# Winograd quarter products of a ConvFFN up-projection: two chain tiles kept in the residual's room, and a new order of the products

## The chip, the cores and the metric

The kernel runs on one core of a Trainium2 chip. The metric is the device time of one execution in microseconds (us). A time is compared as the median of several runs; the profiled execution is one run among them and has a time of its own.

## The reference, cut to what matters

Two post-norm layers over x of shape (512, 1024), float32. Each layer has a mixer (attention-like heads in layer 0, state-space heads in layer 1), then a gated ConvFFN. The change lies in the ConvFFN and its surroundings:

```python
def conv_ffn(x, w_up, conv_w, conv_b, w_down):
    h = causal_dwconv(x @ w_up, conv_w, conv_b)      # w_up (1024, 2*2816), conv of width 3
    val, gate = jnp.split(h, 2, axis=-1)
    return (jax.nn.silu(gate) * val) @ w_down        # w_down (2816, 1024)

x = layer_norm(ALPHA * x + y, ln1_g[layer], ln1_b[layer])     # y: the mixer's output
f = conv_ffn(x, ffn_w_up[layer], ffn_conv_w[layer], ffn_conv_b[layer], ffn_w_down[layer])
x = layer_norm(ALPHA * x + f, ln2_g[layer], ln2_b[layer])
```

## The kernel before, in words

Every float32 product is made of three passes of rounded parts: a weight block of 128x1024 is loaded (by SP's queue), split into `hi` (ScalarE, `ACT hi L285`) and `lo` = block - hi (VectorE, `DVE lo L286`), and TensorE multiplies hi x hi, lo x hi and hi x lo of the activations. `hi` and `lo` come from pools of five buffers each (`wp`), plainly loaded blocks from a pool of four (`raw`, in `rp`).

The up-projection of one layer makes 22 pairs of 128 columns (a gate tile g and a value tile v for each j from 0 to 21), in `up_quarters`. j = 0 and 1 are plain: `gated(j, ...)` calls `mtile` twice (24 matmuls of 512 columns each), then `conv` (one ScalarE pass, two VectorE passes, line L988) and the gate. After that come seven groups. A group is two j made together by a Winograd scheme (seven quarter products in place of eight, 24 matmuls of 256 columns each, line L1055), followed by one plain j (not after the last group). In the groups A11, A12, A22 are quarters of the activations; E, S2, S3, S4 are sums of quarters, made once at the start of the stage (E and S2 by VectorE; S3 and S4 by GpSimd at lines L1027 to L1033 and then split).

The weights of four of the seven products are sums of quarter blocks W11, W12, W21, W22. They are summed by accumulating DMAs that GpSimd issues (`nc.gpsimd.dma_start(c, ..., accum_op=add)`): one tile `c` goes through W11, +W12, +W22, +W21, and each addition may start only when the sum before it is split. The tile `c` has one buffer (tag "t", which the tile of S2 and S4 shares), so the W11 of the next group is loaded when the last sum of this one is split. A second sum, d = W12 + W22, uses one of the four `raw` buffers. Products of a group in order: c=W11 with A11 (PSUM x), W21 with A12, c+W12 with E (PSUM y, held to the end), c+W22 with S2 (added onto x in PSUM), c+W21 with A22 (its own PSUM banks tp and av), d with S3 (onto x), W22 with S4 (onto y). Then comes the plain j.

`proj_ln` makes the mixer's output projection, the residual sum and the layer norm, in four row blocks t; the residual stays in four SBUF tiles `xk` (tag "x" of `rp`) until the down-projection adds to it. The norm of each t has two small GpSimd steps (L314, L315). The down-projection, also `proj_ln`, takes each activation block split by `two` into tiles `s` of a pool that is opened when the up-projection's pool is closed.

The order on each engine is made at build time by a scheduler; each engine runs its instructions strictly in that order, so an instruction that waits holds all that stand behind it.

Of the kernel before, what the change touches and what calls it, by code (L numbers as in the profile page):

```python
# [8 lines left out]
F32 = mybir.dt.float32  # L9
F32R = mybir.dt.float32r  # L10
AF = mybir.ActivationFunctionType
# [95 lines left out]
def trunk(ctx: ExitStack, tc: tile.TileContext, W, x, xT, cols, rows, poolw, consts, out):  # L107
# [15 lines left out]
    def nm(s):  # L123
        uid[0] += 1
        return f"{s}_{uid[0]}"

    def ps(tag="mm"):
        return pp.tile([P, 512], F32, tag=tag, name=nm(tag), bufs={"mm": 4, "S": 2, "tp": 1, "av": 1}[tag])
# [43 lines left out]
    def wraw():  # L172
        return rp.tile([P, D], F32, tag="raw", name=nm("raw"), bufs=4)
# [139 lines left out]
    def rpow(dst, var):  # L313
        G.tensor_scalar(dst, var, EPS, None, ALU.add)  # L314
        return G.tensor_tensor(dst, dst, phalf.to_broadcast(list(dst.shape)) if dst.shape[-1] > 1 else phalf, ALU.pow)  # L315

    def proj_ln(acts, korder, blk, ln, nxt, needs=None, scale=None):


# [85 lines left out]
        for t in range(NT):  # L405
            if t + 1 < ahead:
                last(t + 1)
            elif t >= ahead:
                last(t)
            mv = small([P, 2])  # L410
            V.bn_aggr(mv, st[t][:, 0:4 if fine(t) else 2].rearrange("p a b -> p (a b)"))  # L411
            rs = small([P, 1])
            last_pow = rpow(rs, mv[:, 1:2]).ins
            for h in range(2):
                z = xk[t][:, h * 512:(h + 1) * 512]
                V.scalar_tensor_tensor(z, z, mv[:, 0:1], gain[h], ALU.subtract, ALU.mult)
                for c in (slice(0, 256), slice(256, 512)) if fine(t) and h else (slice(0, 512),):
                    V.scalar_tensor_tensor(z[:, c], z[:, c], rs, shift[h][:, c], ALU.mult, ALU.add)  # L418
                    if nxt is None:
                        nc.sync.dma_start(out[t * P:(t + 1) * P, h * 512 + c.start:h * 512 + c.stop], z[:, c])  # L420
            if nxt is None:
                continue
            if t == NT - 1:

                xcur = xnew
                hi, lo, raw = wload(nxt)
                o = ps()
                mpass(o, hi, lo, 3 * P)
            xf = []
            for h in range(2):  # L430
                z = xk[t][:, h * 512:(h + 1) * 512]
                tp = ps()
                for k in range(4):
                    T.transpose(tp[:, k * P:(k + 1) * P], z[:, k * P:(k + 1) * P], ident)
                split(tp.rearrange("p (a b) -> p a b", b=P), xnew[h][:, :, t * P:(t + 1) * P],
                      xnew[2 + h][:, :, t * P:(t + 1) * P])
                if t == NT - 1:
                    xf.append(tmp())
                    A.activation(xf[h], tp, AF.Copy)
# [540 lines left out]
    def ffn(pool, layer, up, dn, last):  # L980
        cw, cb = C_FW[layer], C_FB[layer]
        act = [pool.tile([P, 2, S], F32, tag="a", name=nm("a"), bufs=NJ // 2) for _ in range(NJ // 2)]

        def conv(j, o):
            c = tmp()
            A.activation(c, o, AF.Identity, bias=c1(cb + j), scale=c1(cw + 2 * 2 * NJ + j))  # L986
            for d in range(1, 3):
                V.scalar_tensor_tensor(c[:, d:], o[:, :S - d], c1(cw + (2 - d) * 2 * NJ + j), c[:, d:],  # L988
                                       ALU.mult, ALU.add)
            return c  # L990

        def gated(j, g, v):
            gt = conv(NJ + j, g())
            A.activation(gt, gt, AF.Silu)
            vl = conv(j, v())
            V.tensor_tensor(act[j // 2][:, j % 2, :], vl, gt, ALU.mult)

        with tc.tile_pool(name=f"up{layer}", bufs=1, side="left") as work:
            up_quarters(work, up, gated)
        after_ln[:] = [None, 0]  # L1000
        with tc.tile_pool(name=f"dn{layer}", bufs=1, side="left") as work:
            def two(b):
                hi, lo = (work.tile([P, 2, S], F32R, tag="s", name=nm("s"), bufs=11) for _ in range(2))
                split(act[b], hi, lo, G)
                return [(hi[:, i, :], lo[:, i, :]) for i in range(2)]
            proj_ln(two, range(NJ), dn, 2 * layer + 1, None if last else OD)

    def up_quarters(pool, up, gated):
# [36 lines left out]
        def wsplit(p):  # L1045
            hi = wp.tile([P, D], F32R, tag="hi", name=nm("hi"), bufs=5)
            lo = wp.tile([P, D], F32R, tag="lo", name=nm("lo"), bufs=5)
            split(p, hi, lo)
            return hi, lo

        def mul(o, w, half, a, start=True):
            n = 0
            for ww, part in ((w[0], 0), (w[1], 0), (w[0], 1)):
                for k in range(4):
                    T.matmul(o[:, L], ww[:, half * 512 + k * P:half * 512 + (k + 1) * P], a[part][:, k, :],  # L1055
                             start=start and n == 0, stop=n == 11, skip_group_check=not start)
                    n += 1

        for j in range(3, NJ, 3):
            js = (j - 1, j)  # L1060
            W11, W12, W21, W22 = (W[up + 2 * (j - 1) + i] for i in range(4))
            if j == 3:
                for i in range(4):
                    sl = slice(i, i + 1)
                    total(G, e[:, sl], [(1, [a[:, sl] for a in A11]), (-1, [a[:, sl] for a in A21])])
                    split(e[:, sl], *(a[:, sl] for a in S3))
                S4 = wide("e", F32R), wide("f", F32R)
                for i in range(4):
                    sl = slice(i, i + 1)
                    more(G, s2[:, sl], s2[:, sl], [a[:, sl] for a in A12], ALU.subtract)  # L1070
                    split(s2[:, sl], *(a[:, sl] for a in S4))
            c = pool.tile([P, D], F32, tag="t", name=nm("t"), bufs=1)
            nc.sync.dma_start(c, W11)
            e21, d, e22 = wraw(), wraw(), wraw()
            nc.sync.dma_start(e21, W21)
            nc.sync.dma_start(d, W12)
            nc.sync.dma_start(e22, W22)
            nc.gpsimd.dma_start(d, W22, accum_op=ALU.add)  # L1078
            g = [pool.tile([P, S], F32, tag="g", name=nm("g"), bufs=2) for _ in js]
            v = [pool.tile([P, S], F32, tag="v", name=nm("v"), bufs=2) for _ in js]  # L1080
            x = [ps("S") for _ in js]
            w = wsplit(c)
            for i in range(2):
                mul(x[i], w, i, A11)
                A.activation(g[i][:, L], x[i][:, L], AF.Copy)
            nc.gpsimd.dma_start(c, W12, accum_op=ALU.add)
            w = wsplit(e21)
            for i in range(2):
                o = ps()
                mul(o, w, i, A12)  # L1090
                V.tensor_tensor(g[i][:, L], g[i][:, L], o[:, L], ALU.add)
            w = wsplit(c)
            y = [ps() for _ in js]
            for i in range(2):
                mul(y[i], w, i, E)
                A.activation(v[i][:, R], y[i][:, L], AF.Copy, scale=-1.0)
            nc.gpsimd.dma_start(c, W22, accum_op=ALU.add)
            w = wsplit(c)
            for i in range(2):
                mul(x[i], w, i, S2, False)  # L1100
                A.activation(v[i][:, L], x[i][:, L], AF.Copy)
            nc.gpsimd.dma_start(c, W21, accum_op=ALU.add)
            w = wsplit(c)
            for i in range(2):
                o = ps(("tp", "av")[i])
                mul(o, w, i, A22)
                A.activation(g[i][:, R], o[:, L], AF.Copy)
            w = wsplit(d)
            for i in range(2):
                mul(x[i], w, i, S3, False)  # L1110
                V.tensor_tensor(g[i][:, R], g[i][:, R], x[i][:, L], ALU.add)
                V.tensor_tensor(v[i][:, R], v[i][:, R], x[i][:, L], ALU.subtract)
            w = wsplit(e22)
            for i in range(2):
                mul(y[i], w, i, S4, False)
                V.scalar_tensor_tensor(v[i][:, L], v[i][:, L], -1.0, y[i][:, L], ALU.mult, ALU.subtract)
                gated(js[i], lambda: g[i], lambda: v[i])
            if j + 1 < NJ:
                gated(j + 1, lambda: mtile(up + 2 * j + 2), lambda: mtile(up + 2 * j + 3))

    with tc.tile_pool(name="ev", bufs=1, side="left") as pool:
        even_mixer(pool)
# [119 lines left out]
```

## Time and profile before

| | before |
|---|---|
| median of 3 runs | 1319.55 us (1314.46 to 1319.63) |
| the profiled execution's own time | 1314.97 us |
| its span, first to last instruction | 1313.2 us |
| TensorE (PE) matmuls busy | 1182.9 us, 90% |
| VectorE (DVE) busy | 835.2 us, 64% |
| ScalarE (ACT) busy | 563.1 us, 43% |
| GpSimd (POOL) busy | 327.9 us, 25% |
| mean granted TensorE clock | 0.943 of full |

The granted clock has two levels, 1.2 and 2.4 GHz (0.5 and 1.0). Times on the profile's timeline count from the span's start. The two up-projections lie at about 270 to 563 us (layer 0) and 870 to 1169 us (layer 1).

### The profile page before, as it was taken

The numbers are of one execution on the slowest core, as the hardware profiler recorded it, in microseconds if no ns is written. First come the engines' busy times: TensorE is split into PE (matmuls) and PEld (weight loads), VectorE is DVE, ScalarE is ACT, GpSimd is POOL, SyncE is SP. The second block draws the span as 40 slices with busy tenths as digits, with TensorE's granted clock in tenths as the row PEclk, the third lists the DMA queues.
The fourth block names the chain that finished last, engine by engine and source line by source line (L and its number), as shares of the span: only waits on it lengthen the run. The fifth ranks groups of instructions, "written<-read, shape, count | busy, mean of one in ns | idle before, by whom it ended". The sixth has DMA issues, their size and how long they took to land. (4 is left out here: it accounts for less than half of the span.)

```text
span 1313.2 us, 16580 instructions
## 1 busy us (share of the span) xinstructions
PE 1182.9 (90%) x6320; PEld 1009.4 (77%) x6320; DVE 835.2 (64%) x1282; ACT 563.1 (43%) x889; POOL 327.9 (25%) x330
## 2 busy tenths in 40 slices
PE   8999999994989898969999999996789889959997
PEld 6777788874878888858887766775778889858886
DVE  5977565693656665654547978596456576663545
ACT  4456532142444544453324477224444345453330
POOL 1223222152000110154422075035101110106442
PEclk9999999997989898979999999997789899989999
DMA  8323422233656555543323242313555556652311
GB/s 283 111 91 106 144 72 83 62 81 64 153 153 161 141 137 129 120 149 96 97 64 121 63 147 65 113 33 88 131 119 132 140 150 156 154 157 75 97 49 64
DMA packets 45648, 149.34 MB, mean 114 GB/s; under 512 B 5096, under 2 KB 5736, under 8 KB 45568
## 3 DMA queue, kind: packets, MB, share of 16 engines
q1 hardware_dynamic: 37344, 118.38, 27.5%
q0 software_dynamic: 8224, 29.89, 13.2%
q8 instruction: 50, 0.82, 0.2%
q14 instruction: 30, 0.25, 0.1%
HBM read 146.11 MB, written 2.15 MB: 113 GB/s over the span
## 5 line engine op out<-in xcount | busy, mean ns | idle before, releaser
L286 DVE TENSOR_TENSOR lo<-raw,hi 128x1024 fp32r<-128x1024 f32 (+1 forms) x187 | 250.8, 1356 | 157.2 <-ACT hi L285 157.0
L238 PE MATMUL mm<-xT,hi 128*128 128x512 f32 (+1 forms) x1088 | 281.7, 400 | 0.5 <-ACT xT L285 0.5
L285 ACT ACTIVATE hi<-raw 128x1024 fp32r<-128x1024 f32 (+1 forms) x189 | 186.2, 996 | 190.8 <-PE mm L334 110.5
L238 PEld LDWEIGHTS mm<-xT,hi 128*128 128x128 f32 x1088 | 201.9, 191 | 44.6 <-issue 4.4
L286 DVE TENSOR_TENSOR lo<-t,hi 128x1024 fp32r<-128x1024 f32 x56 | 68.6, 1225 | 194.4 <-ACT hi L285 194.4
L286 POOL TENSOR_TENSOR s<-a,s 128x1024 fp32r<-128x1024 f32 x44 | 107.2, 2446 | 142.0 <-PE mm L334 72.9
L334 PE MATMUL mm<-hi,s 128*128 128x512 f32 (+1 forms) x396 | 121.6, 387 | 22.7 <-ACT s L285 20.3
L285 ACT ACTIVATE hi<-t 128x1024 fp32r<-128x1024 f32 x56 | 59.5, 1062 | 189.9 <-DMA t<-in_W 189.9
L238 PE MATMUL mm<-xT,lo 128*128 128x512 f32 (+1 forms) x544 | 138.8, 391 | 0.0
L238 PEld LDWEIGHTS mm<-xT,lo 128*128 128x128 f32 x544 | 101.0, 188 | 21.4 <-issue 1.9
L334 PEld LDWEIGHTS mm<-hi,s 128*128 128x128 f32 x396 | 75.4, 194 | 38.5 <-issue 20.6
L1055 PE MATMUL S<-o,hi 128*128 128x256 f32 x448 | 76.3, 308 | 6.6 <-ACT hi L285 6.6
L334 PE MATMUL mm<-lo,s 128*128 128x512 f32 (+1 forms) x198 | 76.4, 386 | 0.0
L1055 PEld LDWEIGHTS S<-o,hi 128*128 128x128 f32 x448 | 68.9, 219 | 7.3 <-ACT hi L285 7.3
L1055 PE MATMUL mm<-o,hi 128*128 128x256 f32 x224 | 44.6, 335 | 32.3 <-DVE tmp L988 29.0
L1055 PEld LDWEIGHTS mm<-o,hi 128*128 128x128 f32 x224 | 38.3, 239 | 34.5 <-issue 30.7
L1078 POOL DMA_DIRECT2D raw<-in_W x14 | 12.3, 876 | 192.6 <-DMA raw<-in_W 74.3
L1055 PE MATMUL S<-xT,hi 128*128 128x256 f32 x224 | 36.6, 300 | 24.6 <-ACT hi L285 24.6
L334 PE MATMUL S<-hi,s 128*128 128x512 f32 x176 | 56.9, 390 | 0.0
L314 POOL TENSOR_SCALAR small<-small 128x1 f32<-128x1 f32 (+2 forms) x25 | 14.5, 579 | 163.1 <-DVE small L411 101.7
L1055 PEld LDWEIGHTS S<-xT,hi 128*128 128x128 f32 x224 | 33.3, 208 | 26.4 <-ACT hi L285 25.5
L988 DVE SCALAR_TENSOR_TENSOR tmp<-mm,col,tmp 128x511 f32<-128x511 f32 (+1 forms) x64 | 47.2, 745 | 7.9 <-ACT tmp L986 7.4
(296 smaller groups left out, 2322.9 us busy)
## 6 DMA issues: line engine op xcount, KB each, us to landing
raw<-in_W SPq DMA_DIRECT2D x176, 512.0 KB, 4.1
t<-in_W POOLq DMA_DIRECT2D x42, 512.0 KB, 5.4
raw<-in_W POOLq DMA_DIRECT2D x14, 512.0 KB, 6.8
t<-in_W SPq DMA_DIRECT2D x14, 512.0 KB, 3.4
bc<-dr SPq DMA_DIRECT2D x20, 256.0 KB, 3.9
tmp<-in_rows SPq DMA_DIRECT2D x16, 256.0 KB, 4.1
raw<-in_W SPq DMA_DIRECT2D x8, 256.0 KB, 5.8
xk<-in_x SPq DMA_DIRECT2D x4, 512.0 KB, 5.8
```

Of the source, the lines that this page charges most:

```text
L238: T.matmul(o[:, :cols_], w[:, k * P:(k + 1) * P], xs_(xcur, part, k)[:, :cols_], start=n == 0, stop=n == 3 * NK - 1)
L285: A.activation(hi, src, AF.Copy)
L286: (lo_eng or V).tensor_tensor(lo, src, r32(hi), ALU.subtract)
L314: G.tensor_scalar(dst, var, EPS, None, ALU.add)
L334: T.matmul(o[:, c], a[:, t * P:(t + 1) * P], ww[:, kk * 512 + c.start:kk * 512 + c.stop], start=first and kk == 0 and n == 0, stop=fin and ...
L988: V.scalar_tensor_tensor(c[:, d:], o[:, :S - d], c1(cw + (2 - d) * 2 * NJ + j), c[:, d:], ALU.mult, ALU.add)
L1055: T.matmul(o[:, L], ww[:, half * 512 + k * P:half * 512 + (k + 1) * P], a[part][:, k, :], start=start and n == 0, stop=n == 11, skip_group ...
L1078: nc.gpsimd.dma_start(d, W22, accum_op=ALU.add)
```

## The change

The chain tile c and the sum d move from the up-projection's pool and from `raw` into the tag "x" of `rp`, the four buffers in which the residual lay. A group takes two of the four, so two groups' chains can stand side by side. The residual is written to a DRAM tensor `away` by SP as each row block's norm is done, and loaded back for the down-projection. The plain j moves from behind the group into its middle, between the product with E and that with S2. The product with A22 becomes the last of the group and is added onto x in PSUM, after S2 and S3, so that PSUM makes a sum that VectorE made (L1111 goes; the banks tp and av are not used). The first two activation blocks of the down-projection are split into `hi`/`lo` buffers of `wp` and not into tiles `s`.

```diff
+    away = dp.tile([NT, P, D], F32, name="away")
 ...
             if nxt is None:
                 continue
+            if needs:
+                nc.sync.dma_start(away[t], xk[t])
 ...
         after_ln[:] = [None, 0]
+        for t in range(NT):
+            xk[t] = rp.tile([P, D], F32, tag="x", name=nm("xk"), bufs=4)
+            nc.sync.dma_start(xk[t], away[t])
         with tc.tile_pool(name=f"dn{layer}", bufs=1, side="left") as work:
+            early = [0, 1]
+
             def two(b):
-                hi, lo = (work.tile([P, 2, S], F32R, tag="s", name=nm("s"), bufs=11) for _ in range(2))
+                if early:
+                    early.pop()
+                    hi, lo = (wp.tile([P, D], F32R, tag=g, name=nm("s"), bufs=5).rearrange("p (a b) -> p a b", a=2)
+                              for g in ("hi", "lo"))
+                else:
+                    hi, lo = (work.tile([P, 2, S], F32R, tag="s", name=nm("s"), bufs=11) for _ in range(2))
 ...
-            c = pool.tile([P, D], F32, tag="t", name=nm("t"), bufs=1)
+            c, d = (rp.tile([P, D], F32, tag="x", name=nm("c"), bufs=4) for _ in range(2))
             nc.sync.dma_start(c, W11)
-            e21, d, e22 = wraw(), wraw(), wraw()
+            e21, e22 = wraw(), wraw()
+            nc.sync.dma_start(d, W12)
             nc.sync.dma_start(e21, W21)
-            nc.sync.dma_start(d, W12)
             nc.sync.dma_start(e22, W22)
 ...
             nc.gpsimd.dma_start(c, W22, accum_op=ALU.add)
+            if j + 1 < NJ:
+                gated(j + 1, lambda: mtile(up + 2 * j + 2), lambda: mtile(up + 2 * j + 3))
             w = wsplit(c)
             for i in range(2):
                 mul(x[i], w, i, S2, False)
                 A.activation(v[i][:, L], x[i][:, L], AF.Copy)
             nc.gpsimd.dma_start(c, W21, accum_op=ALU.add)
-            w = wsplit(c)
-            for i in range(2):
-                o = ps(("tp", "av")[i])
-                mul(o, w, i, A22)
-                A.activation(g[i][:, R], o[:, L], AF.Copy)
             w = wsplit(d)
             for i in range(2):
                 mul(x[i], w, i, S3, False)
-                V.tensor_tensor(g[i][:, R], g[i][:, R], x[i][:, L], ALU.add)
                 V.tensor_tensor(v[i][:, R], v[i][:, R], x[i][:, L], ALU.subtract)
             w = wsplit(e22)
             for i in range(2):
                 mul(y[i], w, i, S4, False)
                 V.scalar_tensor_tensor(v[i][:, L], v[i][:, L], -1.0, y[i][:, L], ALU.mult, ALU.subtract)
+            w = wsplit(c)
+            for i in range(2):
+                mul(x[i], w, i, A22, False)
+                A.activation(g[i][:, R], x[i][:, L], AF.Copy)
                 gated(js[i], lambda: g[i], lambda: v[i])
-            if j + 1 < NJ:
-                gated(j + 1, lambda: mtile(up + 2 * j + 2), lambda: mtile(up + 2 * j + 3))
```

Where the instructions stand now. First place: GpSimd's queue from the last norm step of layer 0's mixer to the end of the first group. `raw_2784` is the d of before, `t_2781` its c; a DMA row of GpSimd is an accumulating DMA. Before:

```order
L191 TENSOR_TENSOR lo_2604<-raw_2601,hi_2603 128x1024
L1078 DMA raw_2784<-in_W 128x1024
L1027 TENSOR_TENSOR e_2650<-xT_2348 128x256 x2
L1029 TENSOR_TENSOR e_2650<-e_2650,xT_2350 128x256 x4
...
L1033 TENSOR_TENSOR t_2651<-t_2651,xT_2351 128x256 x2
L1086 DMA t_2781<-in_W 128x1024
L1097 DMA t_2781<-in_W 128x1024
L1102 DMA t_2781<-in_W 128x1024
L1078 DMA raw_3114<-in_W 128x1024
```

And of the change, in the same place (`c_2786` is the c of the first group, `c_2787` its d, `c_3113` the d of the second):

```order
L1092 DMA c_2787<-in_W 128x1024
L314 TENSOR_SCALAR small_2531<-small_2529 128x1
L315 TENSOR_TENSOR small_2531<-small_2531,phalf 128x1
L191 TENSOR_TENSOR lo_2609<-raw_2606,hi_2608 128x1024
L1092 DMA c_3113<-in_W 128x1024
L1100 DMA c_2786<-in_W 128x1024
L1041 TENSOR_TENSOR e_2655<-xT_2349 128x256 x2
...
L1111 DMA c_2786<-in_W 128x1024
L1046 TENSOR_TENSOR t_2656<-t_2656,xT_2350 128x256 x2
...
L1118 DMA c_2786<-in_W 128x1024
L1092 DMA c_3437<-in_W 128x1024
```

The first d now stands ahead of the last row block's two norm steps, and c's additions stand ahead of and among the sums of quarters, not behind them.

Second place: ScalarE where one group gives way to the next, in the middle of layer 0's up-projection. `g` and `v` are the group's outputs, `S` the PSUM tile x, `mm` a plain tile or y. Before (group with `t_3767`, then that with `t_4095`):

```order
L1101 ACTIVATE v_3779<-S_3781 128x256
L285 ACTIVATE hi_4061<-raw_4059 128x1024
L1107 ACTIVATE g_3776<-tp_3913 128x256
L1107 ACTIVATE g_3777<-av_3927 128x256
L285 ACTIVATE hi_4110<-t_4095 128x1024
L285 ACTIVATE hi_4141<-raw_4097 128x1024
L986 ACTIVATE tmp_3990<-g_3776,col 128x512
```

And of the change (`c_3760` is this group's chain, `c_4084` the next one's; `raw_4195` is the next plain g tile's weights):

```order
L990 ACTIVATE tmp_3938<-mm_3913,col 128x512
L285 ACTIVATE hi_4099<-c_4084 128x1024
L1117 ACTIVATE v_3771<-S_3773 128x256
L1117 ACTIVATE v_3772<-S_3774 128x256
L285 ACTIVATE hi_4130<-raw_4087 128x1024
L285 ACTIVATE hi_4162<-c_4084 128x1024
L285 ACTIVATE hi_4197<-raw_4195 128x1024
L1130 ACTIVATE g_3769<-S_3773 128x256
L990 ACTIVATE tmp_4051<-g_3769,col 128x512
L990 ACTIVATE tmp_4056<-v_3771,col 128x512
L1130 ACTIVATE g_3770<-S_3774 128x256
```

The next chain's W11 and its first sum (W11+W12, `hi_4162`) are now split while this group's S2 to A22 products run, and the copy of this group's last x (L1130) stands behind that second split.

Third place: ScalarE from the last copies of layer 0's last group to the down-projection. Before:

```order
L1107 ACTIVATE g_4761<-av_4911 128x256
...
L986 ACTIVATE tmp_5002<-v_4763,col 128x512
L994 ACTIVATE tmp_4974<-tmp_4974 128x512
L285 ACTIVATE hi_5157<-raw_5155 128x1024
L994 ACTIVATE tmp_4997<-tmp_4997 128x512
L285 ACTIVATE s_5021<-a_2587 128x1024
L285 ACTIVATE s_5059<-a_2588 128x1024
```

And of the change:

```order
L285 ACTIVATE hi_4934<-c_4732 128x1024
L285 ACTIVATE hi_5002<-raw_5000 128x1024
L285 ACTIVATE s_5006<-a_2592 128x1024
L285 ACTIVATE hi_5040<-raw_5038 128x1024
L285 ACTIVATE s_5044<-a_2593 128x1024
L1130 ACTIVATE g_4741<-S_4745 128x256
...
L998 ACTIVATE tmp_4974<-tmp_4974 128x512
L285 ACTIVATE hi_5108<-raw_5106 128x1024
L285 ACTIVATE hi_5142<-raw_5140 128x1024
L285 ACTIVATE s_5078<-a_2594 128x1024
```

Two weight blocks and two activation blocks of the down-projection are split ahead of the last group's last copies; the third activation block stands behind them.

## Rows read from the trace of the kernel before

**Rows 1.** The page's chain that ended last, shares of the span by line

```profile
DMA t<-in_W 9%; PE mm L334 5%; PE S L334 2%; DVE lo L286 2%; DMA raw<-in_W 2%; ACT hi L285 1%; PE tp L334 1%; PE S L1055 1%; DVE tmp L988 1%; PE mm L1055 0%; PE av L334 0%; PE tp L1055 0%; PE av L1055 0%; DVE xk L418 0%; POOL raw L1078 0%
```

**Rows 2.** DMA queues (packets, MB, share) and issues (xcount, size, us to landing)

```profile
q1 hardware_dynamic: 37344, 118.38, 27.5%
q0 software_dynamic: 8224, 29.89, 13.2%
...
raw<-in_W SPq DMA_DIRECT2D x176, 512.0 KB, 4.1
t<-in_W POOLq DMA_DIRECT2D x42, 512.0 KB, 5.4
...
out<-xk SPq DMA_DIRECT2D x7, 256.0 KB, 2.0
```

**Rows 3.** Timeline of PE, layer 1: start us, us, instruction [idle before <-releaser]

```profile
912.20 1.44 PE L1055 MATMUL S<-xT,hi 128*128 128x256 f32 x5 [12.50 <-ACT hi L285]
...
960.25 0.64 PE L1055 MATMUL S<-xT,hi 128*128 128x256 f32 x4
```

**Rows 4.** Timeline of PE, one middle group of layer 1

```profile
1045.28 1.20 PE L1055 MATMUL mm<-o,hi 128*128 128x256 f32 x4 [4.46 <-DVE tmp L988]
...
1057.40 0.64 PE L1055 MATMUL mm<-e,hi 128*128 128x256 f32 x4
...
1060.28 2.00 PE L238 MATMUL mm<-xT,hi 128*128 128x512 f32 x8
...
1071.19 0.64 PE L1055 MATMUL S<-xT,hi 128*128 128x256 f32 x4
```

**Rows 5.** The chain in order of time, same group: start us, us, what

```profile
1060.34 9.45 DMA t<-in_W
...
1070.96 1.24 DVE lo L286
...
1072.48 5.54 DMA t<-in_W
```

**Rows 6.** Windows: stretch us, busy by engine (x), PEclk, DMA share, GB/s

```profile
400.00:410.00 10.00, 7.61 (x59) 7.02 (x59) 6.00 (x8) 4.28 (x8) 0.87 (x1) 1.00 0.33 54
471.00:481.00 10.00, 8.04 (x55) 7.87 (x54) 4.64 (x7) 4.02 (x6) 0.87 (x1) 0.83 0.32 53
1040.00:1050.00 10.00, 5.54 (x30) 5.36 (x30) 3.99 (x6) 2.99 (x5) 0.85 (x1) 0.66 0.39 66
1041.00:1079.00 38.00, 33.26 (x216) 31.19 (x216) 23.23 (x32) 18.06 (x27) 3.44 (x4) 0.91 0.56 139
...
1179.50:1186.50 7.00, 5.79 (x13) 4.12 (x14) 0.00 (x0) 4.62 (x5) 7.00 (x4) 0.51 0.41 143
```

**Rows 7.** Timeline of PE, start of layer 1's down-projection

```profile
1179.48 0.76 PE L334 MATMUL mm<-hi,s 128*128 128x512 f32 x1 [10.08 <-ACT s L285]
```

**Rows 8.** Timeline of PE, the same three places of layer 0

```profile
307.30 1.44 PE L1055 MATMUL S<-xT,hi 128*128 128x256 f32 x5 [12.15 <-ACT hi L285]
...
354.14 0.64 PE L1055 MATMUL S<-xT,hi 128*128 128x256 f32 x4
...
573.17 0.77 PE L334 MATMUL mm<-hi,s 128*128 128x512 f32 x1 [10.22 <-ACT s L285]
```

**Rows 9.** Timeline of DVE and POOL, layer 1's norm and sums of quarters

```profile
862.86 1.41 DVE L418 SCALAR_TENSOR_TENSOR xk<-xk,small,tmp 128x512 f32<-128x512 f32 x2
...
873.96 0.78 POOL L314 TENSOR_SCALAR small<-small 128x1 f32<-128x1 f32 x1 [4.70 <-DVE small L411]
...
904.96 1.40 POOL L1033 TENSOR_TENSOR t<-t,xT 128x256 f32<-128x256 f32 x2
```

**Rows 10.** Timeline of ACT and DVE, a plain tile's conv passes and an x copy

```profile
1042.34 0.76 ACT L986 ACTIVATE tmp<-mm,col 128x512 f32<-128x512 f32 x1
...
1043.60 1.53 DVE L988 SCALAR_TENSOR_TENSOR tmp<-mm,col,tmp 128x511 f32<-128x511 f32 x2
...
1055.09 0.40 ACT L1107 ACTIVATE g<-tp 128x256 f32<-128x256 f32 x1
```

## The prediction

> **What bounds the kernel now.** I read the chain that ended last first: its largest entry is the accumulating DMAs of the chain tile, `t<-in_W` with 9% [rows 1], and in order of time a middle group is one string of addition, split, addition, split [rows 5]. An addition lands 5.54 us after its issue, but 9.45 us when it is issued together with d's [rows 5]; from its landing the ScalarE split and its hand-over take 1.17 us (1069.79 to 1070.96), the VectorE split 1.24, and 0.28 pass until the next addition's issue. With one tile c, the next group's W11 is loaded only when this string is over. So I read TensorE's timeline next, and split each layer's up-projection into three stretches.
>
> First group with its plain j, S1: from the end of j = 1 (912.20 less the 12.50 waited, 899.70) to the next group's first product at 960.25, 60.55 us in layer 1 [rows 3]; in layer 0, 295.15 to 354.14, 58.99 us [rows 8]. Last, the start of the down-projection, S3: TensorE waits 10.08 and 10.22 us [rows 7, 8] and then has 5.79 of 7.00 us busy at half clock [rows 6], so it loses 1.21 us more by waiting and 5.79 x 0.49 = 2.8 by the clock: 14.1 and 14.2 us (layer 0's tail taken as layer 1's). Between them lie groups two to seven, S2: 960.25 to 1169.40 and 354.14 to 562.95, 209.15 and 208.81 us [rows 3, 7, 8].
>
> What S1 and S2 would take if TensorE never waited: a product is 24 matmuls, 2.88 us (1057.40 to 1060.28), a plain j 10.91 (1060.28 to 1071.19) [rows 4]. A group with a plain j is 7 x 2.88 + 10.91 = 31.07 us; S2 has 42 products and five plain j, 175.5 us. So S2 loses 33 us per layer and S1 28 to 29. Each loss shows its cause: in S1 the first c is loaded late, in S2 a wait such as the 4.46 us for a PSUM bank that VectorE's `tmp` pass frees, because that pass stands behind a split that waits for c [rows 4]. The waits also cost clock. In 400 to 410, idle 2.39 us in pieces, the granted clock stayed at 1.00; with 1.96 idle it fell to 0.83, with 4.46 to 0.66 over the 10 us [rows 6], which is 1.7 and 3.4 us lost.
>
> **The first group.** c no longer shares a tile with S2 and S4 and is loaded as soon as the first residual block is away, so the 12 us wait goes. What is late next is S4 and the passes behind it. GpSimd ends its sums of quarters at 906.36 before [rows 9]. It starts them when VectorE has split E, and VectorE now has two weight splits (1.24 each [rows 5]) and four conv passes (1.53 for two [rows 10]) ahead of that, 5.5 us in all; I put GpSimd's end that much later, at 911.9. ScalarE's last copy of S4 and a g copy (0.40 each [rows 10]), then VectorE's adds, free PSUM for the plain tile at about 913.4. TensorE could begin it at 899.7 + 3 x 2.88 = 908.3, so it waits 5.1 us, and I charge 2.2 for the clock, between 1.7 and 3.4. S1 becomes 31.07 + 7.3 = 38.3 us (bounds 32 and 45): **20.7 and 22.2 us less**.
>
> **The middle groups.** Here the plain j hides the addition before S2, and the next c is loaded early. The steps that are left in a row run from the end of the plain j to the next group's first product, which on TensorE are four products, 11.52 us. On the other engines: the conv's ScalarE pass 0.76, two VectorE passes 1.53 [rows 10], the split of the next W11, 1.24, and 0.28 to the issue, the addition of W12, 5.54, ScalarE's split of it 1.17 [rows 5], the next plain tile's `hi`, by the same rows about 1.1, and only then, in ScalarE's order, the copy that frees x, 0.40 [rows 10]: 12.0 us, 0.5 more than TensorE needs. The second half of x follows two conv passes of ScalarE later, which costs some 0.3 more than the product's half of 1.44 covers. So a boundary costs **at least 0.8 us**. At most the addition takes 9.45 us, as it does beside d's: 3.9 more, and with a fall of the clock by 3.4 us it is 8.1. I take 0.9 more for the addition, since SP issues d's load only after the plain tile's, which waits for a buffer that the split before S4 gives back some 12 us into the group; d then lands near 19 us, its addition leaves at about 20 and c's at 23, an overlap of part of the way. Of the clock I add 0.8, half of what the wait of 1.96 us lost, since this wait of 1.7 is a little shorter. That is 2.5 us per boundary, five boundaries, and 1 us in the last group, which has no plain j: S2 takes 175.5 + 13.5 = 189 us, **19.8 and 20.2 less**.
>
> Do the other engines fit a group of 33 to 34 us? VectorE had 23.23 us and ScalarE 18.06 us in 38 [rows 6]; yes. The DMA engines: plain loads took 27.5% of the span for 118.38 MB, 1.6 us per 512 KB of all sixteen, additions 13.2% for 29.89 MB, 3.0 us [rows 2]. Six loads and four additions make 21.7 us of 33.5, so they fit, if not without queueing.
>
> **The down-projection's start.** ScalarE's `s` split waited for the room of the old pool. Now two weight and two activation blocks are split before the last copies, so 48 matmuls (11 us) stand ready; the third activation block needs a weight buffer turned over at 5.6 us, two ScalarE passes and a GpSimd pass, about 11 us, just in time. I charge 1 us (bounds 0 and 5): **13.1 and 13.2 less**.
>
> **What is added.** Per layer four blocks go out and come back: 256 KB lands in 2.0 us, 512 KB of load in 4.1 [rows 2], and nothing but c and d waits for them. c's cover is wide (it is needed at 899.7). d's is thin: its addition stands on GpSimd ahead of the norm step that starts at 873.96 [rows 9]. The second block's norm ends at 864.27 [rows 9]; write and load at 4.1 each bring d at 872.5. That holds by 1.5 us; each us beyond holds the norm, and TensorE behind it, by as much. With one ScalarE split in front of a transposed block I charge 0.5 per layer (bounds 0 and 2). Reloading happens under the down-projection, whose residual is first read after half its products. The two PSUM adds less per group (0.8 us of VectorE) are not on a path: nothing.
>
> **The sum.** 20.7 + 22.2 + 19.8 + 20.2 + 13.1 + 13.2 - 1.0 = 108.2 us off the profiled execution's 1314.97: 1206.8. Its time is 4.6 us under the median of the runs shown, whose spread is 5.2; I leave half of that and forecast **1209 us**.
>
> **Rivals.** *No wait is left* (additions at 5.54, S1 at 36, the start free): boundaries at 0.8 make S2 179.5, the sum 23 + 24.5 + 29.3 + 29.6 + 14.2 + 14.1 - 1 = 134, **1181 us**. For it: the boundary is short by only 0.5; against it: more transfers fall together than before.
>
> *The additions meet other transfers at every boundary.* Each boundary costs 8.1, S2 217, and S1 40: 19 + 20.5 - 8.2 - 7.9 + 26.3 - 1 = 49 us, **1266**. The 9.45 us row speaks for it, the order of SP's loads against it. The Trainium skill, page DMA: Bandwidth & Descriptors, section Issuing engines are not separate DMA queues, says that transfers started by different engines run on the same 16 DMA engines and interleave. By that rule, loads that now come earlier do not come for nothing; the 5.54 and 9.45 us agree with it.
>
> *The second tile does not help*, because splits can run only five products ahead, whatever is loaded: S2 stays as it was, 108.2 - 40 = 68.2 us of the sum stay, **1247**.
>
> *Slower than before*: GpSimd's queue. d's addition of the next group stands ahead of c's; if d's load comes late, every c waits for it, and so does each group. The saving elsewhere is 68.2 us and S2 loses 67 now, so it turns at (68.2 + 67 - 2) / 10 = 13.3 us per boundary, that is with d landing some 14 us later than I place it. At 15, **1332 us**. Only SP's order stands against it: one load that waits for a buffer holds d.
>
> **Chances and range.** The forecast (1188 to 1230) 0.50, no wait 0.18, meeting transfers 0.13, no help 0.07, slower 0.05; 0.07 is left for what I don't see (0.02 faster, 0.04 the same, 0.01 slower). Half a per cent is about what a measurement of this kernel can tell from no change. Faster by more than that: 0.50 + 0.18 + 0.13 + 0.07 + 0.02 = 0.90; the same 0.04; slower 0.06. The range 1174 to 1264 holds the forecast, the third case, most of the first rival and nearly half of the second: about 0.8.
>
> **What would show it.** Right: the first group's wait of 12 us is gone and the second group starts 36 to 40 us after j = 1; the groups come every 32 to 35 us; between A22 and the next A11 a wait of 1 to 2 us, ended by ScalarE's copy to g; the first L334 product without a wait; `c<-in_W` landing in 5.5 to 7 us. Wrong: waits of 4 us at each boundary with additions of 9 us; a GpSimd wait for d's load ahead of c's addition; the last norm step held by d; a wait at the third block of the down-projection.

## The result, and the profile of the changed kernel

The changed kernel takes 1278.4 us (median of 4 runs, 1272.7 to 1282.55), the kernel before on the same chip 1318.0. The ratio is 0.970, with a 95% interval of 0.965 to 0.975: faster by some 40 us, of a forecast 108, and outside the range of 1174 to 1264. Its profiled execution took 1282.55 us with a span of 1280.5, against 1314.97 and 1313.2.

The page of the changed kernel: the start of its chain by line, three kinds of DMA issue, and the costliest group of quarter products (busy, mean ns of one | idle before, and its main releaser). Its first line and its DMA issues answer to [rows 1, 2].

```profile
DMA c<-in_W 7%; PE mm L336 4%; PE mm L238 3%; PE S L1069 3%; PE mm L1069 2%; PE S L336 2%; DVE lo L286 1%; PE tp L336 1%; ACT hi L285 1%; DVE tmp L992 1%; POOL e L1043 1%; PE av L336 0%; POOL e L1041 0%; DMA raw<-in_W 0%; POOL s L286 0%
...
L1069 PE MATMUL S<-xT,hi 128*128 128x256 f32 x448 | 85.1, 333 | 57.2 <-ACT g L1130 52.3
...
raw<-in_W SPq DMA_DIRECT2D x162, 512.0 KB, 3.7
c<-in_W POOLq DMA_DIRECT2D x56, 512.0 KB, 7.1
c<-in_W SPq DMA_DIRECT2D x28, 512.0 KB, 3.9
```

The additions are still the chain's largest entry. Their median is now 7.1 us, c's and d's together; before, c's alone had 5.4, and d's stood in another row of the page. 52.3 us of TensorE's idle time stand in one group: the products A11 and A22, waiting for ScalarE's copy out of x.

Now TensorE's timeline at the ends of the three stretches (start us, us, instruction [idle before <-releaser]), first of layer 0, then of layer 1. They answer to [rows 3, 4, 7, 8].

```profile
294.71 0.52 PE L1069 MATMUL S<-xT,lo 128*128 128x256 f32 x3
...
343.88 0.58 PE L1069 MATMUL S<-xT,hi 128*128 128x256 f32 x1 [6.17 <-ACT g L1130]
...
557.05 0.51 PE L336 MATMUL mm<-hi,s 128*128 128x512 f32 x1
...
886.40 0.40 PE L1069 MATMUL S<-xT,lo 128*128 128x256 f32 x2
...
901.61 1.20 PE L1069 MATMUL mm<-o,hi 128*128 128x256 f32 x4 [8.81 <-DVE tmp L992]
...
933.66 0.58 PE L1069 MATMUL S<-xT,hi 128*128 128x256 f32 x1 [6.25 <-ACT g L1130]
...
1011.12 1.22 PE L1069 MATMUL S<-xT,hi 128*128 128x256 f32 x4 [5.37 <-ACT g L1130]
...
1120.59 1.12 PE L1069 MATMUL S<-xT,hi 128*128 128x256 f32 x8
...
1144.86 0.40 PE L336 MATMUL mm<-hi,s 128*128 128x512 f32 x1
...
1156.64 0.50 PE L336 MATMUL mm<-hi,s 128*128 128x512 f32 x1 [0.69 <-ACT s L285]
...
1160.58 0.73 PE L336 MATMUL mm<-hi,s 128*128 128x512 f32 x2 [3.20 <-POOL s L286]
```

The wait of 12 us for the first c is gone, and so are the 10 us at the down-projection. The groups, however, come 37.8 to 39.1 us apart (343.88 to 498.08 and 933.66 to 1087.35), and at the first five of the six boundaries between groups of each layer TensorE waits 3.8 to 6.3 us, 52.3 in all ten. At the last boundary of each layer, between groups six and seven, it does not wait: the row at 1120.59 holds A22 and A11 back to back. With these rows, and those of the kernel named in the last column, the stretches are:

| stretch, us | before | forecast | after | experiment 2 |
|---|---|---|---|---|
| S1, layer 0 | 58.99 | 38.3 | 49.17 | 40.75 |
| S1, layer 1 | 60.55 | 38.3 | 47.26 | 41.96 |
| S2, layer 0 | 208.81 | 189 | 213.17 | 185.31 |
| S2, layer 1 | 209.15 | 189 | 211.20 | 184.90 |
| end of layer 0's S2 to end of layer 1's j = 1 | 336.75 | 324.0 | 329.35 | 331.13 |
| end of layer 1's S2 to the end | 143.8 | 130.7 | 135.64 | 135.6 |

S2, which was to lose 40 us, has grown by 6.4. What holds a boundary is plain from the chain in order of time around the wait at 1011.12, to be held against [rows 5]:

```profile
998.55 0.54 POOL c L1092
999.09 9.63 DMA c<-in_W
1008.72 0.02 issue
...
1008.80 1.06 ACT hi L285
...
1011.41 6.43 DMA c<-in_W
```

and from the timelines of GpSimd, SP and VectorE of the same stretch. L1092 is d's addition, L1100 c's of W12, L1118 c's of W21; L1089 is d's load; `lo<-c` at 993.09 is the split for A22, at 996.54 that of the next group's W11.

```profile
984.38 0.86 POOL L1118 DMA_DIRECT2D c<-in_W  x1 [10.91 <-DVE lo L286]
998.55 0.86 POOL L1092 DMA_DIRECT2D c<-in_W  x1 [13.30 <-DVE a L1000]
999.09 1.22 POOL L1100 DMA_DIRECT2D c<-in_W  x1
...
1037.36 0.86 POOL L1092 DMA_DIRECT2D c<-in_W  x1 [12.86 <-DMA c<-in_W]
1037.89 1.22 POOL L1100 DMA_DIRECT2D c<-in_W  x1
...
994.34 0.33 SPq L1089 DMA_DIRECT2D c<-in_W  x1
...
993.09 1.23 DVE L286 TENSOR_TENSOR lo<-c,hi 128x1024 fp32r<-128x1024 f32 x1 [1.90 <-ACT hi L285]
...
996.54 1.21 DVE L286 TENSOR_TENSOR lo<-c,hi 128x1024 fp32r<-128x1024 f32 x1
```

The d that is loaded at 994.34, and whose addition leaves at 998.55, belongs to the group after next. The four buffers go round two groups, and they are given out in the order in which they come free: the next-but-one c takes the buffer of this group's d, and the next-but-one d that of this group's c, which comes free only when c has been split for A22, at 994.32. d's load leaves 0.02 us later and takes 3.9 us in the median, and only then does its addition leave (at the next boundary, 1037.36, the row names the load as what it waited for), 0.54 us ahead of c's, which stands behind it on GpSimd. c's addition then takes 9.63 us and not 5.5. W11 of the next group had been split by 997.75: without d, the addition could have landed at about 1003.5. Groups six and seven have no d two groups on, and their boundary has no wait.

### The profile page after: what moved, and what is told of

Its sections match the earlier page's. It is cut to its first block, busy times and chain, and to the rows that moved or that the text cites. A ratio compares the mean times of both kernels' runs of the same rounds, so it can differ in the third digit from the quotient of the medians.

```text
span 1280.5 us, 16455 instructions
## 1 busy us (share of the span) xinstructions
PE 1169.7 (91%) x6320; PEld 1000.5 (78%) x6320; DVE 838.7 (65%) x1254; ACT 563.0 (44%) x889; POOL 335.0 (26%) x330
## 5 line engine op out<-in xcount | busy, mean ns | idle before, releaser
L286 DVE TENSOR_TENSOR lo<-raw,hi 128x1024 fp32r<-128x1024 f32 (+1 forms) x173 | 239.6, 1390 | 128.1 <-ACT hi L285 127.5
L285 ACT ACTIVATE hi<-raw 128x1024 fp32r<-128x1024 f32 (+1 forms) x175 | 172.2, 989 | 168.2 <-PE mm L336 102.4
L286 DVE TENSOR_TENSOR lo<-c,hi 128x1024 fp32r<-128x1024 f32 x70 | 84.3, 1220 | 123.1 <-ACT hi L285 123.1
L285 ACT ACTIVATE hi<-c 128x1024 fp32r<-128x1024 f32 x70 | 73.7, 1056 | 183.6 <-DMA c<-in_W 175.1
L286 POOL TENSOR_TENSOR s<-a,s 128x1024 fp32r<-128x1024 f32 x44 | 119.0, 2719 | 108.0 <-PE mm L336 54.5
L1069 PE MATMUL S<-xT,hi 128*128 128x256 f32 x448 | 85.1, 333 | 57.2 <-ACT g L1130 52.3
L1069 PEld LDWEIGHTS S<-xT,hi 128*128 128x128 f32 x448 | 75.3, 240 | 60.1 <-ACT g L1130 54.4
L992 DVE SCALAR_TENSOR_TENSOR tmp<-mm,col,tmp 128x511 f32<-128x511 f32 (+1 forms) x64 | 47.3, 747 | 51.0 <-ACT tmp L990 50.0
L1069 PE MATMUL S<-o,hi 128*128 128x256 f32 x448 | 65.3, 283 | 1.2 <-ACT v L1117 1.2
L990 ACT ACTIVATE tmp<-mm,col 128x512 f32<-128x512 f32 x32 | 24.6, 776 | 67.7 <-PE mm L238 58.8
L1092 POOL DMA_DIRECT2D c<-in_W x14 | 12.3, 880 | 150.2 <-DMA c<-in_W 62.6
```

Source lines behind the costliest of these rows:

```text
L285: A.activation(hi, src, AF.Copy)
L286: (lo_eng or V).tensor_tensor(lo, src, r32(hi), ALU.subtract)
```

## The experiments

Theory A: the loss comes from d's addition, which stands one place ahead of c's on GpSimd. Rivals: B, two additions in flight slow each other whichever is first; C, the plain loads around it slow c's addition. Every ratio is to runs of the kernel before on the same chip in the same session.

### 1 and 2. d's addition behind c's

`issue_after` queues an instruction behind another of its engine. In the first kernel that is c's addition of W12 of one group on, in the second that of W22; the loads stay as they were.

```diff
-            nc.gpsimd.dma_start(d, W22, accum_op=ALU.add)
+            if j == 3:
+                nc.gpsimd.dma_start(d, W22, accum_op=ALU.add)
+            else:
+                with tc.issue_after(last.ins):
+                    nc.gpsimd.dma_start(d, W22, accum_op=ALU.add)
...
-            nc.gpsimd.dma_start(c, W12, accum_op=ALU.add)
+            last = nc.gpsimd.dma_start(c, W12, accum_op=ALU.add)
```

> The only edit: on GpSimd, d's addition is issued just behind c's addition of W12, no longer just ahead of it; buffers, loads and their order stay. Theory A (the ten waits of 3.8 to 6.3 us between a group's last product and the next group's first, 52 us in all, and the 3.4 us of half clock behind each, come from c's addition sharing its flight with d's, and the one issued first is served first): c's addition lands in 5.5 to 7 us, the waits shrink to 0 to 2 us, and the time is 1200 to 1225 us. Rival B (two additions in flight share the engines, whichever is first): c's addition still takes 8.5 to 10 us, the waits stay at 4 to 6 us, and the time is 1265 to 1285. Rival C (c's addition is slow from the plain loads around it, not from d's): as B here, and the next two kernels change nothing either.

> The only edit: on GpSimd, d's addition is issued behind c's addition of W22, some 8 us after that of W12. Under theory A and under rival B alike c's addition of W12 now flies alone: 5.5 to 7 us, waits of 0 to 2 us at the ten boundaries, 1200 to 1225 us, while d's addition meets that of W22, which the plain j hides. Rival C (plain loads slow c's addition): waits of 4 to 6 us stay, 1260 to 1285 us. A third outcome, waits of 4 us moved to the product with S2, would give 1240 to 1270.

Measured: 1226.6 us, ratio 0.927 (0.924 to 0.930), 1.6 us above the range that I gave theory A, and 1217.1 us, 0.921 (0.920 to 0.923), inside it. The first kernel's chain and GpSimd's timeline (L1104 is c's addition of W12, L1096 d's):

```profile
992.43 5.54 DMA c<-in_W
...
992.43 0.86 POOL L1104 DMA_DIRECT2D c<-in_W  x1 [11.62 <-DVE lo L286]
993.49 0.86 POOL L1096 DMA_DIRECT2D c<-in_W  x1 [0.20 <-issue]
```

and the second's (L1115 is c's addition of W22):

```profile
981.64 5.39 DMA c<-in_W
...
989.73 5.59 DMA c<-in_W
...
989.73 0.86 POOL L1115 DMA_DIRECT2D c<-in_W  x1 [7.22 <-DVE lo L286]
990.27 1.22 POOL L1096 DMA_DIRECT2D c<-in_W  x1
```

With d's addition 1.06 or 0.54 us behind it, c's takes 5.54 and 5.59 us; with d's 0.54 us ahead it took 9.63. Rival B falls: the first one issued is not slowed. Rival C falls for this addition: one plain load leaves just behind it in all three kernels, at 999.77 in the changed one (0.7 us behind) and at 993.90 and 983.35 in these (1.5 and 1.7). Plain loads do cost where three of them surround an addition; the last section has the figures. In the second kernel the group `S<-xT,hi` has 9.9 us idle where it had 57.2.

### 3. d in the buffer that comes free early

```diff
-            nc.sync.dma_start(c, W11)
             e21, e22 = wraw(), wraw()
             nc.sync.dma_start(d, W12)
+            nc.sync.dma_start(c, W11)
```

> The only edit: d's load is issued where c's was and c's where d's was, so that d takes the buffer that the d of two groups before gave back early, and c the one that c gave back last. GpSimd's order stays: d's addition ahead of c's of W12. Theory A: d lands some 9 us earlier, its addition leaves before the boundary and c's flies alone; the waits shrink to 0 to 2.5 us (a plain load now begins where d's began), 1200 to 1230 us. Rival C: the transfer that starts 5 us ahead of c's addition is a load of the same size as before, so c's addition stays slow, 1260 to 1285 us.

Measured: 1234.7 us, 0.934 (0.930 to 0.939), 4.7 us above the range. The order on GpSimd is the old one, but d's addition (L1092) now leaves 4.5 us ahead of c's:

```profile
954.62 0.87 POOL L1092 DMA_DIRECT2D c<-in_W  x1 [7.04 <-DMA c<-in_W]
959.11 0.86 POOL L1100 DMA_DIRECT2D c<-in_W  x1 [3.62 <-DVE lo L286]
...
959.11 7.11 DMA c<-in_W
```

c's takes 7.1 us, and boundaries wait 0 to 3 us. So it is not the order alone, but the order together with a buffer that came free late; undoing either brings most of the gain.

### 4. No addition to d

The diff takes out the line of d's addition.

> d's addition is left out altogether, so the product with S3 uses W12 alone and the output is another one; everything else stays. It is the bound of what d's addition costs: theory A 1195 to 1220 us, the waits at the ten boundaries 0 to 2 us; rival C 1255 to 1280 us with waits of 4 us or more.

Measured: 1214.3 us, 0.919 (0.917 to 0.921); the output is another one, since S3's weights lack W22. That is the bound of all that d's addition can cost, and moving it behind W22's reaches it within 0.002.

### 5. One tile, all else as changed

```diff
-            c, d = (rp.tile([P, D], F32, tag="x", name=nm("c"), bufs=4) for _ in range(2))
+            c = pool.tile([P, D], F32, tag="t", name=nm("t"), bufs=1)
             nc.sync.dma_start(c, W11)
-            e21, e22 = wraw(), wraw()
+            e21, d, e22 = wraw(), wraw(), wraw()
+            nc.sync.dma_start(e21, W21)
             nc.sync.dma_start(d, W12)
-            nc.sync.dma_start(e21, W21)
```

and the residual stays where it was (the lines that write it out and load it back are taken out; not shown).

> The change without its first part: c in the one tile of before and d in a staging buffer, the residual stays in the chip's memory; the plain pair amid the group, the sum left to PSUM and the down-projection's start are as in the changed kernel. Theory A (the second tile lets the next W11 and its addition come early, and only d's place on GpSimd spoiled that): with one tile the next W11 is loaded only after A22's split, and a load of 3.9 us, splits of 2.3 and an addition of 5.5 stand against A22's 2.9 and two products more: a boundary waits 4 to 9 us, the first group's wait of 12 stays, 1280 to 1335 us. The rival 'the second tile does not help' gives about what the changed kernel takes, 1265 to 1285.

Measured: 1283.0 us, 0.972 (0.969 to 0.974), no different from the changed kernel's 0.970 (0.965 to 0.975). Theory A's range and the rival's both hold this time, so the time alone does not part them; the trace does. Its chain in order of time is one string again: the next W11's load and three additions, each behind its splits.

```profile
963.32 3.52 DMA t<-in_W
...
969.47 5.45 DMA t<-in_W
...
977.62 5.77 DMA t<-in_W
...
989.18 7.49 DMA t<-in_W
```

So the second tile as it was built brought nothing that can be measured, and with d's addition in its right place (experiment 2) it is worth 0.9715 - 0.9214 = 0.050, 66 us. In the kernel with one tile no addition of c stands close behind d's: around 990 us d's leaves 2.9 us behind one of c's. The trace has the waits of 14.0 and 13.8 us before the first product that the second tile takes away. It also has waits of 2.6 to 5.8 us before S2 in each group but the last, where the changed kernel has 1.2 us in all; at the boundaries, where I had expected 4 to 9 us, it waits 0.3 us at most.

### 6. The early activation blocks alone

The kernel before, with `early` and its two weight buffers in `two` as in the change.

> The kernel before with one part of the change alone: the first two activation blocks of each down-projection are split into the weights' buffers. The prediction's term is 13.1 and 13.2 us less, which would give a ratio of 0.980 and 1290 to 1296 us; by the changed kernel's trace, where the down-projections came only 9.4 and 8.2 us shorter because a third block waits on GpSimd, a ratio of 0.985 to 0.989, 1300 to 1306 us.

Measured: 1298.4 us, 0.982 (0.979 to 0.985), 21 us less, between the two sizes.

### 7 and 9. The place of the plain pair, and of the product with A22

Both start from experiment 2's kernel. The first puts `gated(j + 1, ...)` back to the group's end, the second puts A22 back behind S2, in banks of its own and with VectorE's additions.

> As the kernel with d's addition behind that of W22, but with the plain pair back at the group's end. Theory A: the plain pair is what covers the addition before S2 (5.4 us and two splits), and at the end it covers more than the boundary needs: some 5 to 8 us of waiting before S2 in each of fourteen groups, with 2 to 3 us of clock, against half a microsecond saved at each boundary, 1290 to 1350 us. Rival: with two tiles the place of the plain pair no longer matters, 1210 to 1235 us.

> As the kernel with d's addition behind that of W22, but the product with A22 stands where it stood before the change: behind the product with S2, in PSUM banks of its own, with VectorE's two additions. The addition of W21 is then wanted 2.9 us after its own start instead of 8.6 us. Theory A, in which every addition of 5.4 us with its two splits of 2.3 needs about 7.7 us of other products: TensorE waits some 4 to 5 us in each of the fourteen groups with 1.5 to 3 us of clock, 1280 to 1325 us. Rival: the place of this product is free, as the prediction charged for the PSUM sum, 1214 to 1225 us.

Measured: 1232.0 us, 0.933 (0.930 to 0.936), and 1247.1 us, 0.947 (0.945 to 0.949), against 0.921. Both places matter, 16 and 33 us by the ratios, but theory A as I had put it gave at least 73 and 63: the first time lies in its rival's range, the second in neither. In the first kernel the wait before S2 is 1.2 to 1.8 us past the first group, not 5 to 8: with two tiles W12's addition leaves before the plain pair begins, and W22's before A11 does (GpSimd, L1104 and L1115):

```profile
962.21 0.87 POOL L1104 DMA_DIRECT2D c<-in_W  x1 [13.35 <-DVE lo L286]
973.74 0.86 POOL L1115 DMA_DIRECT2D c<-in_W  x1 [10.67 <-DVE lo L286]
```

while the plain pair's first matmul is at 965.15 and its last eight begin at 974.25. So with the plain pair at the end, too, the additions are started that far ahead.

In the second kernel the product with A22 does not wait for W21's addition, except in the last group (5.3 and 3.1 us). What waits is the second half of the next group's first product, 1.6 to 4.2 us, and the chain of one such boundary ends on VectorE:

```profile
976.78 5.17 DMA c<-in_W
...
983.06 1.23 DVE lo L286
984.29 0.33 DVE g L1131
984.62 0.34 DVE v L1132
```

The split of the next chain's first sum holds VectorE, and behind it stand the two passes that free x; one of them, L1131, is the addition that the change had given to PSUM. No run parts the place of the product from that addition.

### 8. S4's sums on VectorE

Experiment 2's kernel still waits 8.8 us in layer 1's first group. There VectorE's timeline has a pass that is twelve times as long as the same one just before, and GpSimd's, under it, four rows of sums, of which the first and the last stand here. The lines are the changed kernel's, which shows the same:

```profile
892.44 0.50 DVE L286 TENSOR_TENSOR o<-e,o 128x256 fp32r<-128x256 f32 x1 [3.17 <-ACT o L285]
893.14 6.07 DVE L286 TENSOR_TENSOR o<-e,o 128x256 fp32r<-128x256 f32 x1 [0.20 <-ACT o L285]
...
899.73 0.74 DVE L992 SCALAR_TENSOR_TENSOR tmp<-mm,col,tmp 128x511 f32<-128x511 f32 x1
...
893.19 1.68 POOL L1046 TENSOR_TENSOR t<-t,xT 128x256 f32<-128x256 f32 x2
...
897.28 1.64 POOL L1047 TENSOR_TENSOR t<-t,xT 128x256 f32<-128x256 f32 x2
```

```diff
-                    more(G, s2[:, sl], s2[:, sl], [a[:, sl] for a in A12], ALU.subtract)
+                    more(V, s2[:, sl], s2[:, sl], [a[:, sl] for a in A12], ALU.subtract)
```

> As the kernel with d's addition behind that of W22, but the eight sums that make S4's input run on VectorE and not on GpSimd. Theory H: in the first group a VectorE pass of 0.50 us took 6.06 while GpSimd ran its sums back to back, and the conv pass behind it held the PSUM bank that TensorE waited 8.8 us for; without GpSimd's sums that pass is short again, the sums cost VectorE about 3.3 us, TensorE's wait falls to 2 to 5 us in layer 1, and the time by 4 to 12 us, to 1205 to 1213 us. Rival K: the long pass is only a wait for data that the record shows as work, and the sums on VectorE hold the conv pass as long: 1214 to 1222 us.

Measured: 1220.6 us, 0.924 (0.921 to 0.928): no gain over 0.921, and in rival K's range. The long pass is gone, though; in VectorE's timeline of this kernel the same two passes are

```profile
861.03 0.50 DVE L286 TENSOR_TENSOR o<-e,o 128x256 fp32r<-128x256 f32 x1 [3.16 <-ACT o L285]
861.72 0.43 DVE L286 TENSOR_TENSOR o<-e,o 128x256 fp32r<-128x256 f32 x1 [0.20 <-ACT o L285]
```

So GpSimd's sums did hold that pass (rival K's reason falls), but TensorE's wait of 8.8 us only became two, of 3.3 and 3.5. Before the second, S4's parts come behind ScalarE's split of c, which in the new order stands ahead of theirs and starts when W22's addition has landed, at 866.6. Half the theory stands, and the gain that I drew from it does not.

### 10 and 11. Splits of the activation, and S3's sums, on VectorE

```diff
-                split(act[b], hi, lo, G)
+                split(act[b], hi, lo, G if b > 2 else None)
```

The second kernel also has `total(V, e[:, sl], ...)` for S3's sums.

> As the kernel with d's addition behind that of W22, but the low halves of the first three activation blocks of each down-projection are made by VectorE and not by GpSimd. Theory H (VectorE's and GpSimd's passes hold each other up: 1.22 and 0.74 us became 2.78 and 2.56 while two GpSimd passes took 6.4): the waits at the start of the down-projection, 3.9 us with 3.4 to 6.8 us at half clock, and part of the 0.8 to 2.2 us in the last group go, 2 to 6 us per layer, 1205 to 1213 us. Rival K: three more VectorE passes of 1.22 us delay the last conv as much, 1214 to 1221 us.

> As the kernel just before, and the sums that make S3's input run on VectorE too, so that GpSimd can start on S4's without waiting for them. Theory: GpSimd's string of 18.4 us behind the split of E is what the first group waits for; without S3's 12 us TensorE's wait of 4.4 to 8.8 us falls to 0 to 4 and the clock's 10 us at half with it, 3 to 8 us per layer below the kernel just before, 1193 to 1206 us. Rival: VectorE, which has four conv passes and two weight splits in the same stretch, gives S3 no earlier and is itself held by GpSimd's sums: no better than the kernel just before, 1206 to 1220 us.

Measured: 1205.5 us, 0.914 (0.911 to 0.917), and 1206.7 us, 0.915 (0.914 to 0.917). The first is the fastest kernel of this study, and its interval lies below experiment 2's. TensorE's wait at layer 1's third activation block, 0.69 + 3.20 us in the changed kernel, is

```profile
1087.13 0.73 PE L336 MATMUL mm<-hi,s 128*128 128x512 f32 x2 [0.86 <-DVE s L286]
```

and the granted clock stays at 1.00 there. Moving S3's sums as well changes nothing: layer 1's long wait goes (8.8 us become 0.8 and 1.8), but waits of 1.2 to 2.8 us stand elsewhere, and its rival holds.

## Why the prediction was wrong

**The step that failed** is in S2: "I take 0.9 more for the addition, since SP issues d's load only after the plain tile's, which waits for a buffer that the split before S4 gives back some 12 us into the group; d then lands near 19 us, its addition leaves at about 20 and c's at 23". I asked what d's load waits for on SP, and not whose buffer it goes into. It goes into that of c, which is the last thing the group gives back: 22 us into the group (972.33 to 994.34), with the addition at 26.2 and c's at 26.8. The overlap is whole, not part, at each boundary. The upper bound that I had worked out for it, 8.1 us with the clock, was about what it cost: the eight intervals between these boundaries are 38.5 us in the mean, 7.4 more than the 31.07 of TensorE's work, of which 5.0 are waiting and the rest half clock. The last group added to it: it waits 3.8 and 3.2 us, where I had charged 1. I priced the case rightly from the row of 9.45 us [rows 5] and then argued it away. Experiments 1 to 4 show the cause from four sides.

**S2's size without that step.** In experiment 2 S2 takes 185.3 and 184.9 us; I had said 189. Boundaries there wait 0 to 1.6 us: nearer the bound of 0.8 than the 2.5 that I charged.

**S1** came to 49.2 and 47.3, not 38.3. Without the boundary's wait it is 40.8 and 42.0 us (experiment 2), so 8.4 and 5.3 us of that are the boundary again, for which my 38.3 had no term at all. The rest is S4's wait: GpSimd's sums end 12.5 us after j = 1 in layer 1 (898.92 - 886.40), and I had put them at 12.2. But TensorE already stops amid the product with E (901.61, 8.81 us), not behind it, so the wait was 8.8 us and not 5.1. The granted clock was 0.50 for 10.2 us, of which only the last 3.9 fall on work, some 2 us lost: about the 2.2 that I had charged. Both values of experiment 2 lie within my bounds of 32 and 45.

**S3** gave 8.2 us in layer 1 and, with the norm between, 7.4 in layer 0, not 13. I called the third activation block "just in time" at 1 us. TensorE waits 3.9 us for it, the second part for GpSimd's pass, and runs 3.4 us at half clock. With VectorE splitting it (experiment 10) the stretch to the end is 1205.5 - 1074.7 = 130.8 us: the forecast's 130.7.

**What was right.** The first c's wait went, and the plain pair in its new place has no wait behind it past the first group. Nothing of the new traffic holds the norm: on GpSimd, d's first addition is out of the way before the last norm step, which waits for VectorE,

```profile
854.56 0.95 POOL L1092 DMA_DIRECT2D c<-in_W  x1 [1.76 <-DMA c<-in_W]
856.44 0.22 POOL L314 TENSOR_SCALAR small<-small 128x1 f32<-128x1 f32 x1 [0.94 <-DVE small L413]
```

and the stretch that has the norm is, in experiment 10, 325.96 us (521.59 to 847.55), some 2 more than the terms make it.

**The sum without that step.** The kernel of experiment 2 takes 1217 us and the forecast was 1209, but that is nearer than the terms were: against them S2 takes 8 us less in both layers together, S1 6 more, and the two stretches with the start of the down-projection 12 more.

**A term put at nothing.** I charged nothing for the two PSUM adds less, since they were on no path. In experiment 9, where the addition is back on VectorE and A22 back behind S2, it stands on the path of the boundary shown there, with 0.33 us. A22's new place had no term of its own; with the PSUM sum it is worth 0.025, 33 us.

**The rivals.** The second, additions that meet other transfers at every boundary (1266), had about the right price and the wrong partner: the plain load that meets c's addition at the boundary slows it little (5.39 us at 981.64 in experiment 2). The slower rival had the right partner, d on GpSimd ahead of c, but it was to be slower only from 13.3 us per boundary on. "The second tile does not help" came true in the time (experiment 5), for a reason that I had not named.

## What to carry to other kernels

When buffers of one pool serve two kinds of tile, write down for each load which tile's last reader frees its buffer, and for how many groups ahead the load is: here a load two groups ahead took the one buffer that came free last, and an addition that nobody needed for another 70 us (998.55, for the product with S3 of a group that starts at 1049.57) stood in front of the one that TensorE waited for. On a queue that is served in order, put the transfer that is waited for first; of the two ways to get there, queue order brought all of it and buffer order most. When a gain as large as a second buffer measures as nothing, look for the wait that took its place before dropping the buffer: moving one line was worth 5% here.

## What the runs showed of the hardware

Two accumulating transfers of 512 KB from GpSimd's queue do not share evenly when they leave within about a microsecond of each other: the first lands nearly as if alone (5.54 and 5.59 us; before the change an addition with no other transfer near it, issued at 1043.98, took 5.27), the second after 9.2 to 9.6 in the changed kernel; at a distance of 4.5 us the second takes 7.1 (experiment 3). Plain loads, which SP issues, slow an addition too: W21's, with no other addition ahead of it but three loads of 512 KB issued within 2 us of it, takes 7.14 us (issued at 946.19 in the changed kernel) and 7.65 (at 945.93 in experiment 1). The Trainium skill, page DMA: Bandwidth & Descriptors, section Issuing engines are not separate DMA queues, says that DMAs started by different engines run on the same 16 DMA engines and interleave. The 7.14 and 7.65 us agree with it. For two transfers of one engine the rows show order instead, so the 5.54 and 9.45 us that I set beside that section [rows 5], both of them GpSimd's, were no test of it.

A VectorE pass took 6.07 us, where the same pass just before took 0.50, while GpSimd ran eight sums back to back, and it ended 0.3 us after the last of them; with those sums moved it took 0.43. The Trainium skill, page SBUF — State Buffer, section Who interferes with whom, says that a VectorE instruction with two SBUF inputs contends with a GpSimd instruction that reads SBUF. The trace agrees, and shows one pass held through eight of them.
